# A hybrid decoder layer on one core: more warm-up matmuls, and the first input products ahead of the second half's transposes

## The chip, the cores and the metric

The kernel runs on one core of a Trainium2 chip. The metric is the device time of one execution in microseconds, as the median of the runs shown. The engines are TensorE (PE; its weight loads are listed as PEld), VectorE (DVE), ScalarE (ACT), GpSimd (POOL) and SyncE (SP), whose queue issues the loads from memory here.

## What is computed

One decoder layer on 512 tokens of width 1024, in float32. Two kinds of heads work beside each other, both fed by one input product:

```
h = rms_norm(x, norm_w)                     # (512, 1024)
proj = h @ w_in                             # (512, 4096): hq hf hi hg | aq ak av ag
o_h = rms_norm(hgrn2(hq, hf, hi, lower_bounds)) * silu(hg)     # 4 heads of 128
o_a = moba(aq, ak, av, q_norm_w, k_norm_w) * silu(ag)          # 8 heads of 64
x = x + concat(o_h, o_a) @ w_out
```

HGRN2 is a gated linear recurrence, evaluated in chunks; MoBA is causal attention over blocks of 256 keys with learned choice of past blocks.

## The kernel before

**Products in three parts.** Every float32 product with weights is made of rounded parts: of an operand the kernel keeps a rounded high part and the remainder as a low part (`whi`, `wlo` for weights, `hTh`, `hTl` for the transposed x), and adds high x high, low x high and high x low in PSUM. A chunk of weights is 256 rows by 512 columns (512 KB). ACT makes `whi` (a cast, L109), DVE makes `wlo` (a subtraction, L117). The factor of the RMSNorm over x (`rst`) is put on after the product; `norm_w` is put on at the transposing.

**The opening.** The first group of 512 output columns is `hi`, for which x is the stationary operand: four accumulators, one for each 128 tokens. x comes in by eight loads (128 tokens by 512 columns each) and is transposed on PE. The order on PE in this opening is written out by hand in the string `SEQ` (L128), whose words are:

- `yN`: N matmuls of a 128x128 tile of ones with itself, whose result nobody reads (`warm_up`, L238). Each leaves two records in the trace. The tile they write is one of the two PSUM buffers that the accumulators also use.
- `nt`: `norm_w` into a column, by a small transpose.
- `tAK`: four transposes of x, of token half A (0 is tokens 0 to 255, 1 is 256 to 511) and weight chunk K (256 of the 1024 input columns); behind them two ACT copies of 256 columns into `hTh` (`x_turn`, L248). `lAK` is the pair of DVE instructions for `hTl` (`x_lo`, L261).
- `whK`, `wlK`: the high and the low part of weight chunk K (L105, L113).
- `pUK`: four matmuls of accumulator U (tokens 128 U to 128 U + 127) with `whi` of chunk K; `qUK`: the two with `wlo` (`part`, L832).
- `sqI`: the sum of squares of 128 tokens of x on ACT; `rs`, `rr`: the norm factor, and it as a row; `cv`, `cm`: small constants.

The order on PE is that of the string, word for word. For ACT, DVE and POOL the string is only the order of the program: there a scheduler may let an instruction that is ready earlier go ahead of others. The loads on SP have a string of their own, `DSEQ` (L129): first x of tokens 0 to 255, columns 0 to 511 (`x00`, `x10`), with the first weight chunk (`w0`) behind them, then tokens 256 to 511 (`x20`, `x30`), and so on.

**The rest.** After the opening a planner in the kernel (`drive`) places the other products' matmuls on PE as filler, and between them the steps of the recurrence and of attention, by estimated latencies. The evacuation of the group `av` is `ev_v` (L577): for each 128 tokens one ACT copy into `vt`. Attention comes after it; per unit DVE adds the bias and takes the minimum, ACT applies the exp (L622), DVE takes the reciprocal of the sums (L625), POOL scales (L627), PE transposes. Beside attention runs the output product, whose results DVE adds to x (L697), loaded anew. ACT reads its functions from tables; where the next function isn't in the loaded one, the trace shows an ACT_TABLE_LOAD. `warm` is a tile of one column whose exp has no other use than to have the table loaded.

Of the kernel before, what the change touches and what calls it, by code (L numbers as in the profile page):

```python
# [11 lines left out]
AF = mybir.ActivationFunctionType  # L12
# [9 lines left out]
def kernel(  # L22
# [12 lines left out]
    nc = tc.nc  # L35
# [89 lines left out]

    POOL_LO = (3,)
    LAT = dict(lm=4.544, lev0=9.2567, lev=4.4882, copy=1.9908, rms=5.7036, silu=15.1764, qk=14.2881, soft=2.5598, softn=0.0041, acopy=4.5215, st=1.5748, ch=6.6909, DEPTH=2)
    SEQ = 'y7 nt t00 wh0 t01 sq0 t10 l00 t11 wl0 p00 q00 l01 wh1 p10 q10 l10 p30 q30 wl1 t03 l11 p20 q20 t12 t02 sq1 p01 q01 wh2 l03 l12 sq3 wh3 p21 q21 p11 q11 sq2 l02 p31 q31 wl2 p32 q32 rs wl3 p02 q02 p22 q22 cv t13 p12 q12 rr cm l13'  # L128
    DSEQ = 'x00 nw x10 w0 x20 x30 x01 x31 x11 w1 x21 w2 w4 v w3 w5'  # L129
    POOL_LO = (3,)  # L130
    for w in DSEQ.split():
# [18 lines left out]
    warm = const.tile([P, 1], F32, name="warm")  # L150
# [65 lines left out]
    rst = const.tile([P, NT], F32, name="rst")  # L216
# [328 lines left out]
    A = {}  # L545

    def wait_for(*keys):
        while not all(kk in done for kk in keys):
            advance()
# [27 lines left out]
    def ev_v(u, ps):  # L577
        if u == 0:
            wait_for(*[("read", n) for n in range(NT)])
            A["v"] = big.tile([P, NT, 512], F32, tag="G", name="vt")  # L580
        if u == 1:
            nc.scalar.activation(warm, warm, AF.Exp)
        nc.scalar.activation(A["v"][:, u, :], ps, AF.Copy, scale=rst[:, u:u + 1])


    UNITS = ((3,), (2,), (1, 0))
# [230 lines left out]
    def fill_a():  # L817
        const_tri()
        yield from group(1, True, ev_f)
        yield from group(2, True, ev_silu_t(q2[:, 0]))  # L820
        yield from group(3, False, ev_silu(G))
        yield from group(4, True, ev_silu_t(gT))
        const_dist()
        yield from group(5, False, ev_qk("K", ("f", "k", "i", "KL"), kgs))
        yield from group(6, False, ev_qk("Q", ("q",), qgs))
        yield from group(7, False, ev_v)

    with tc.manual_schedule(engines={mybir.EngineType.PE}):
        with tc.manual_schedule():
# [17 lines left out]
            def part_lo(u, kp):  # L847
# [3 lines left out]
                        wh=split_hi, wl=split_lo)  # L851
            for w in SEQ.split():
                name = w.rstrip("0123456789")
# [58 lines left out]
```

## Time and profile before

| | us |
|---|---|
| median of 3 runs | 296.12 |
| lowest and highest | 296.12 and 297.62 |
| the profiled execution, its own time | 296.24 |
| its span, first to last instruction | 294.5 |
| PE busy | 285.4 (97%) |
| DVE busy | 173.2 (59%) |
| ACT busy | 131.7 (45%) |
| POOL busy | 57.8 (20%) |

The profile is of one execution. Times within it count from the start of the span. A row of a timeline has its start, its duration and its count of merged instructions; what stands in brackets at the end is the idle time of the engine just ahead of the row, with what ended it. Matmuls are pipelined, so a row's duration overlaps the next one; the time of one in a run is the distance of the starts. The granted clock is given as a share of TensorE's full 2.4 GHz; the lower level is 1.2 GHz, 0.50.

### The profile page before, as it was taken

The page shows a single profiled execution, that of the slowest core. Times are in us where ns is not written, and L with a number is a line of the kernel's source. Part 1 is how long each engine was busy: PE and PEld are TensorE (multiplying, and loading weights), DVE is VectorE, ACT ScalarE, POOL GpSimd, SP SyncE. Part 2 cuts the span into 40 slices and gives each one's busy share as a digit, 9 for nine tenths or more (in the row PEclk, how much of TensorE's full clock was granted, in tenths as well). Part 3 has the DMA queues.
Part 4 walks back from the last instruction along what each step waited for, and adds up shares of the span by engine and source line. Part 5 has one row for each costly group of instructions (what it writes and reads, how often), then busy time and mean ns, then how long its engine had stood idle before and what let it go on. Part 6 is the DMA issues. An engine that isn't in the chain of part 4 may idle for free.

```text
span 294.5 us, 5056 instructions
## 1 busy us (share of the span) xinstructions
PE 285.4 (97%) x1945; PEld 236.8 (80%) x1945; DVE 173.2 (59%) x371; ACT 131.7 (45%) x241; POOL 57.8 (20%) x92
## 2 busy tenths in 40 slices
PE   6699999999999999999999999999999999999995
PEld 5588788888877787888888888888887888887884
DVE  4452644464599999446875586485385577633232
ACT  3746654431520456314521653554468697642000
POOL 1003301155000000010254422420004655320000
PEclk9599999999999999999999999999999999999999
DMA  6963276080070006200430089648269000000122
GB/s 202 354 246 129 11 61 250 0 265 21 18 268 6 2 2 198 90 0 0 156 131 1 0 239 185 142 140 226 53 171 341 9 2 0 2 2 2 71 109 105
DMA packets 21642, 31.00 MB, mean 105 GB/s; under 512 B 1509, under 2 KB 8434, under 8 KB 21618
## 3 DMA queue, kind: packets, MB, share of 16 engines
q1 hardware_dynamic: 21618, 30.68, 35.7%
q8 instruction: 15, 0.25, 0.3%
q14 instruction: 9, 0.07, 0.1%
HBM read 25.17 MB, written 2.10 MB: 93 GB/s over the span
## 4 chain that ended last, share of the span: by engine, by line
PE 93%; DMA 5%; SPq 1%; DVE 0%; POOL 0%; issue 0%; DVEq 0%; POOLq 0%
PE acc L173 74%; PE tp L177 7%; PE ot L173 3%; PE sc L173 3%; PE pl L173 3%; DMA x<-in_x_dram 3%; DMA res<-in_x_dram 2%; PE ops L173 2%; PE us L173 1%; SPq L71 0%; DVE res L697 0%; POOL scr L627 0%; SPq L100 0%; DVE res L733 0%; SPq L133 0%
## 5 line engine op out<-in xcount | busy, mean ns | idle before, releaser
L173 PE MATMUL acc<-whi,hTh 128*128 128x512 f32 x160 | 65.4, 409 | 0.0
L173 PE MATMUL acc<-whi,hTl 128*128 128x512 f32 x160 | 63.0, 394 | 0.0
L173 PE MATMUL acc<-wlo,hTh 128*128 128x512 f32 x160 | 60.2, 393 | 0.0
L117 DVE TENSOR_TENSOR wlo<-raw,whi 128x1024 fp32r<-128x1024 f32 x39 | 47.2, 1235 | 13.0 <-ACT whi L109 12.8
L109 ACT CAST whi<-raw 128x1024 fp32r<-128x1024 f32 x40 | 41.5, 1049 | 14.3 <-DMA raw<-in_w_in_dram 6.8
L173 PE MATMUL acc<-hTh,whi 128*128 128x512 f32 x96 | 38.2, 397 | 0.0
L173 PE MATMUL acc<-hTh,wlo 128*128 128x512 f32 x96 | 37.5, 391 | 0.0
L173 PE MATMUL acc<-hTl,whi 128*128 128x512 f32 x96 | 37.4, 389 | 0.0
L163 POOL TENSOR_TENSOR r<-v,mh 128x8 f32<-128x8 f32 (+1 forms) x12 | 17.2, 1430 | 99.5 <-DVE v L161 99.4
L173 PEld LDWEIGHTS acc<-whi,hTl 128*128 128x128 f32 x160 | 30.4, 190 | 6.5
L173 PEld LDWEIGHTS acc<-whi,hTh 128*128 128x128 f32 x160 | 30.5, 191 | 6.3
L173 PEld LDWEIGHTS acc<-wlo,hTh 128*128 128x128 f32 x160 | 30.4, 190 | 5.9
L627 POOL TENSOR_SCALAR scr<-scr,rl 128x512 f32<-128x512 f32 (+3 forms) x32 | 17.7, 564 | 40.7 <-DVE rl L625 37.1
L173 PEld LDWEIGHTS acc<-hTh,wlo 128*128 128x128 f32 x96 | 18.0, 188 | 4.0 <-DVE wlo L117 0.2
L173 PEld LDWEIGHTS acc<-hTl,whi 128*128 128x128 f32 x96 | 18.1, 188 | 3.5
L173 PEld LDWEIGHTS acc<-hTh,whi 128*128 128x128 f32 x96 | 18.0, 188 | 3.6
L173 PE MATMUL acc<-whi,mTa 128*128 128x512 f32 (+1 forms) x72 | 20.4, 367 | 0.0
L697 DVE TENSOR_TENSOR res<-acc,res 128x512 f32<-128x512 f32 x15 | 10.3, 690 | 15.9 <-PE acc L173 14.6
L177 PE MATMUL tp<-ident,scr 128*128 128x128 f32 x128 | 18.6, 276 | 0.4 <-POOL scr L627 0.3
L622 ACT ACTIVATE scr<-scr,nm 128x512 f32<-128x512 f32 (+3 forms) x32 | 17.7, 554 | 2.9 <-DVE nm L619 2.9
L177 PEld LDWEIGHTS tp<-ident,scr 128*128 128x128 f32 x128 | 14.8, 140 | 4.0 <-POOL scr L627 1.1
L619 DVE CUSTOM_DVE_ANT_0 scr<-sc,bias 128x512 f32<-128x512 f32 (+3 forms) x32 | 14.1, 485 | 5.9 <-PE sc L173 5.8
(139 smaller groups left out, 422.0 us busy)
## 6 DMA issues: line engine op xcount, KB each, us to landing
raw<-in_w_in_dram SPq DMA_DIRECT2D x32, 512.0 KB, 4.0
raw<-in_w_out_dram SPq DMA_DIRECT2D x8, 512.0 KB, 3.9
x<-in_x_dram SPq DMA_DIRECT2D x8, 256.0 KB, 7.1
res<-in_x_dram SPq DMA_DIRECT2D x8, 256.0 KB, 6.3
out_dram<-res SPq DMA_DIRECT2D x7, 256.0 KB, 2.1
K<-K SPq DMA_DIRECT2D x8, 128.0 KB, 6.4
KL<-KL SPq DMA_DIRECT2D x8, 128.0 KB, 6.6
Q<-scr SPq DMA_DIRECT2D x8, 128.0 KB, 2.7
```

Source lines behind the costliest of these rows:

```text
L109: nc.scalar.copy(hi, raw)
L117: eng.tensor_sub(lo, raw, hi.bitcast(F32))
L163: nc.gpsimd.tensor_tensor(r, v, mh[:, 0:n], op=ALU.pow)
L173: nc.tensor.matmul(o, a, b, start=start, stop=stop)
L177: nc.tensor.transpose(o, a, ident)
L619: nc.vector.tensor_tensor_reduce(out=z[:, o:o + n], in0=sc[:, o:o + n], in1=bias[:, j, T - n:T], op0=ALU.add, op1=ALU.min, scale=1.0, scal ...
L622: nc.scalar.activation(z[:, o:o + n], z[:, o:o + n], AF.Exp, bias=nm[:, e:e + 1], scale=-1.0, accum_out=l[:, e:e + 1])
L627: nc.gpsimd.tensor_scalar(z[:, o:o + n], z[:, o:o + n], rl[:, e:e + 1], 1.0, op0=ALU.mult, op1=ALU.mult)
L697: nc.vector.tensor_tensor(res[hf][:, u, :], ps, res[hf][:, u, :], op=ALU.add)
```

## The change

Two edits. In `SEQ` the first warm-up grows from 7 to 10 matmuls; one more stands behind the transposes t00 and two behind t01. The words p00 and p10 come ahead of t10, so the first eight products of tokens 0 to 255 stand ahead of the transposes of tokens 256 to 511; q00 stands behind t10, and q10 behind t11. t03 goes behind p20 and q20, and sq0 in the program from behind t01 to behind t03. In `ev_v` the exp on `warm` comes behind the copy of the second tile of `vt` instead of ahead of it, and reads a column of that tile with scale 0.

```
-    SEQ = 'y7 nt t00 wh0 t01 sq0 t10 l00 t11 wl0 p00 q00 l01 wh1 p10 q10 l10 p30 q30 wl1 t03 l11 p20 q20 t12 t02 sq1 p01 q01 wh2 l03 l12 sq3 wh3 p21 q21 p11 q11 sq2 l02 p31 q31 wl2 p32 q32 rs wl3 p02 q02 p22 q22 cv t13 p12 q12 rr cm l13'
+    SEQ = 'y10 nt t00 wh0 y1 t01 l00 y2 p00 wl0 p10 l01 t10 q00 t11 q10 l10 wh1 p30 q30 l11 wl1 p20 q20 t03 sq0 t12 t02 sq1 p01 q01 wh2 l03 l12 sq3 wh3 p21 q21 p11 q11 sq2 l02 p31 q31 wl2 p32 q32 rs wl3 p02 q02 p22 q22 cv t13 p12 q12 rr cm l13'
...
         if u == 0:
             wait_for(*[("read", n) for n in range(NT)])
             A["v"] = big.tile([P, NT, 512], F32, tag="G", name="vt")
+        nc.scalar.activation(A["v"][:, u, :], ps, AF.Copy, scale=rst[:, u:u + 1])
         if u == 1:
-            nc.scalar.activation(warm, warm, AF.Exp)
-        nc.scalar.activation(A["v"][:, u, :], ps, AF.Copy, scale=rst[:, u:u + 1])
+            nc.scalar.activation(warm, A["v"][:, u, 0:1], AF.Exp, scale=0.0)
```

PE at the start of the program, before: x_79 holds tokens 0 to 255 of x, x_80 tokens 256 to 511; `wp` is what the warm-up writes, `tp` what a transpose writes, `acc` an accumulator.

```order
L241 MATMUL wp<-scr 128x128 x7
L245 MATMUL tpn<-ident,vec 128x8
L177 MATMUL tp<-ident,x_79 128x128 x8
L177 MATMUL tp<-ident,x_80 128x128 x8
L173 MATMUL acc<-whi,hTh 128x512
L173 MATMUL acc<-whi,hTl 128x512
```

The same place on PE after the change, up to t11:

```order
L241 MATMUL wp<-scr 128x128 x10
L245 MATMUL tpn<-ident,vec 128x8
L177 MATMUL tp<-ident,x_79 128x128 x4
L241 MATMUL wp<-scr 128x128
L177 MATMUL tp<-ident,x_79 128x128 x4
L241 MATMUL wp<-scr 128x128 x2
...
L173 MATMUL acc<-whi,hTh 128x512
L173 MATMUL acc<-whi,hTl 128x512
L177 MATMUL tp<-ident,x_80 128x128 x4
L173 MATMUL acc<-wlo,hTh 128x512 x2
L177 MATMUL tp<-ident,x_80 128x128 x4
```

The eight matmuls of p00 and p10 (the first six of them are left out) have moved ahead of the transposes of x_80, and the transposes of x_80 now have a pair of `wlo` products between them.

ACT at the start, the difference: `raw_85` holds the first two weight chunks, `raw_94` the third; `sq` is a sum of squares.

```order
 L258 ACTIVATE hTh<-tp,nwc 128x256 x2
+L109 CAST whi<-raw_85 128x1024
+L258 ACTIVATE hTh<-tp,nwc 128x256 x6
 L109 CAST whi<-raw_85 128x1024
 L258 ACTIVATE hTh<-tp,nwc 128x256 x2
 L223 ACTIVATE sq,ssx<-x_79 128x1024
 L258 ACTIVATE hTh<-tp,nwc 128x256 x4
-L109 CAST whi<-raw_85 128x1024
-L258 ACTIVATE hTh<-tp,nwc 128x256 x6
 L223 ACTIVATE sq,ssx<-x_79 128x1024
 L109 CAST whi<-raw_94 128x1024
```

The first sum of squares has moved from ahead of the copies of t10 and t11 to behind the second weight chunk and the copies of t03.

ACT between the group `av` and the first softmax, before:

```order
L583 ACTIVATE vt<-acc,rst 128x512
L535 ACTIVATE Q<-tp,qgs 64x4x128 x2
L583 ACTIVATE vt<-acc,rst 128x512
L535 ACTIVATE Q<-tp,qgs 64x4x128
L109 CAST whi<-raw 128x1024 x3
L583 ACTIVATE vt<-acc,rst 128x512
L109 CAST whi<-raw 128x1024
L622 ACT_TABLE_LOAD
L622 ACTIVATE scr,l<-scr,nm 128x512 x2
```

And after the change, from the second tile of `vt` on:

```order
L581 ACTIVATE vt<-acc,rst 128x512
L535 ACTIVATE Q<-tp,qgs 64x4x128
L583 ACT_TABLE_LOAD
L583 ACTIVATE warm<-vt 128x1
L535 ACTIVATE Q<-tp,qgs 64x4x128
L581 ACTIVATE vt<-acc,rst 128x512
...
L109 CAST whi<-raw 128x1024
L622 ACTIVATE scr,l<-scr,nm 128x512 x2
```

The table load has moved from in front of the first exp of attention to between two copies of Q. On DVE at that place one of the two reciprocals of the second unit has moved ahead of the residual add that they both stood behind. SP's order is the same.

## Rows read from the trace of the kernel before

**Rows 1.** The page, part 1: busy us, share of the span, instructions per engine.
```profile
PE 285.4 (97%) x1945; PEld 236.8 (80%) x1945; DVE 173.2 (59%) x371; ACT 131.7 (45%) x241; POOL 57.8 (20%) x92
```

**Rows 2.** Who PE waited for: us in total, times, longest.
```profile
PE tp L177 <- DMA x<-in_x_dram: 4.3, 3, 3.5
```

**Rows 3.** The chain of waits that ended last: start, us, what.
```profile
2.96 7.57 DMA x<-in_x_dram
...
19.53 0.87 PE tp L177 x8
...
32.20 49.78 PE acc L173 x219
...
120.57 0.89 PE ops L173 x8
```

**Rows 4.** Timeline of PE, 0 to 22 us: start, us, what, idle before.
```profile
1.04 3.35 PE L241 MATMUL wp<-scr 128*128 128x128 f32 x14 [1.04 <-DVE warm L151]
4.32 0.27 PE L245 MATMUL tpn<-ident,vec 8*128 8x8 f32 x1
...
5.20 0.99 PE L177 MATMUL tp<-ident,x 128*128 128x128 f32 x7 [0.33 <-DMA x<-in_x_dram]
9.71 0.45 PE L177 MATMUL tp<-ident,x 128*128 128x128 f32 x1 [3.52 <-DMA x<-in_x_dram]
10.57 1.76 PE L177 MATMUL tp<-ident,x 128*128 128x128 f32 x7 [0.42 <-DMA x<-in_x_dram]
11.98 0.78 PE L173 MATMUL acc<-whi,hTh 128*128 128x512 f32 x1
...
13.84 1.05 PE L173 MATMUL acc<-wlo,hTh 128*128 128x512 f32 x2
14.69 0.47 PE L173 MATMUL acc<-whi,hTh 128*128 128x512 f32 x1
...
20.16 0.47 PE L173 MATMUL acc<-whi,hTh 128*128 128x512 f32 x1
```

**Rows 5.** PE by stretches: from:to, length, PE busy, granted clock, DMA share, GB/s.
```profile
4.50:8.00 3.50, 1.36 (x9) 1.00 0.96 297
8.00:9.70 1.70, 0.00 (x0) 0.51 0.97 311
...
12.00:14.80 2.80, 2.80 (x9) 0.50 0.93 356
14.80:20.20 5.40, 5.40 (x32) 1.00 0.60 206
```

**Rows 6.** Timeline of ACT and DVE in the opening.
```profile
5.79 0.84 ACT L258 ACTIVATE hTh<-tp,nwc 128x256 fp32r<-128x256 f32 x2 [3.34 <-PE tp L177]
...
6.66 0.87 DVE L266 SCALAR_TENSOR_TENSOR hTl<-tp,nwc,hTh 128x256 fp32r<-128x256 f32 x2
...
8.08 1.04 ACT L109 CAST whi<-raw 128x1024 fp32r<-128x1024 f32 x1 [1.46 <-DMA raw<-in_w_in_dram]
...
21.45 1.07 ACT L223 ACTIVATE sq<-x 128x1024 f32<-128x1024 f32 x1
...
22.49 1.06 ACT L109 CAST whi<-raw 128x1024 fp32r<-128x1024 f32 x1
...
23.58 1.23 DVE L117 TENSOR_TENSOR wlo<-raw,whi 128x1024 fp32r<-128x1024 f32 x1 [1.04 <-ACT whi L109]
```

**Rows 7.** Timeline of ACT, DVE and PE around the exp tables and the first softmax.
```profile
2.24 0.20 ACT L582 ACTIVATE warm<-warm 128x1 f32<-128x1 f32 x1
...
209.76 0.68 ACT L535 ACTIVATE Q<-tp,qgs 64x512 fp32r<-64x512 f32 x1 [3.12 <-PE tp L177]
...
220.16 1.28 ACT L622 ACT_TABLE_LOAD   x1
...
224.47 0.69 DVE L697 TENSOR_TENSOR res<-acc,res 128x512 f32<-128x512 f32 x1 [1.30 <-DMA res<-in_x_dram]
...
225.97 1.11 PE L177 MATMUL tp<-ident,scr 128*128 128x128 f32 x6 [0.34 <-POOL scr L627]
```

## The prediction, made before the changed kernel ran

> **What bounds the kernel now.** The page comes first: TensorE (PE) is busy 285.4 us, 97% of the span [rows 1], so only two things can shorten the span: the 9 us in which it stands idle, and work done at a lower clock. The list of who waited for whom says where PE stood: 4.3 us for loads of x [rows 2]; beside that 1.04 us ahead of the first warm-up matmul [rows 4], 0.34 us for GpSimd (POOL) late in the kernel [rows 7], and some 3.4 us at the end, while the last output goes out. The chain of waits confirms it: until 10.53 us the end of the kernel hangs on a load of x, and from there on almost without a break on PE [rows 3]. So whatever moves the first long run of matmuls forward moves the end by as much, unless something behind it is not ready. The timeline shows the opening: the transposes of tokens 0 to 255 (t00, t01) end at 6.19 (5.20 + 0.99), then PE waits 3.52 us and, after one transpose, 0.42 us more for the x rows of tokens 256 to 511; p00 starts at 11.98 [rows 4]. The third view is the granted clock: 1.00 up to 8 us, 0.50 to 14.8, then 1.00 again [rows 5]. It fell about 1.8 us after PE went idle and came back at 14.8, after 2.8 us of unbroken matmuls. Under it a matmul took 0.425 us (two from 13.84 to 14.69) [rows 4] against 0.2273 (49.78 / 219) at the full 2.4 GHz [rows 3], and a transpose 0.201 (10.57 to 11.98 for seven) against 0.109 (0.87 / 8) [rows 3, 4]. The clock view's 1.00 before 4 us I don't trust: 14 warm-up records took 0.234 us each (1.04 to 4.32) [rows 4], where the same 128x128 f32 form takes 0.111 (0.89 / 8) later [rows 3].
>
> So the stretch from 6.19 to the start of p01 at 20.16 lasts 13.97 us, but holds only 24 matmuls and 20 transposes: 24 x 0.2273 + 20 x 0.109 = 5.46 + 2.18 = 7.63 us at full level. Of the 6.3 us above that, 3.9 is waiting and about 2.4 the clock.
>
> **The reordering.** What p00 and p10 need is there before the x rows of tokens 256 to 511: the rounded weight whi of the first chunk is finished by ScalarE (ACT) at 8.08 + 1.04 = 9.12, bound by the load of that chunk, which this change doesn't touch (SP issues the same loads in the same order and waits there for earlier loads only); hTh and hTl of t00 were ready by 7.53 [rows 6]. So p00 can start at about 9.18 and stand where PE now waits. All that follows up to p01 is the same 24 matmuls and 20 transposes. At the full level p01 starts at 9.18 + 7.63 = 16.81. One new hand-over could hold it: p30 needs hTl of t10, which VectorE (DVE) makes after ACT's pair. At full level t10 ends at about 11.6, ACT's pair takes 0.84, DVE's first half 0.44 more [rows 6]: 12.9 to 13.0, and p30 comes up at 9.18 + 12 x 0.2273 + 8 x 0.109 = 12.78, its hTl matmul 0.23 later. That is level, and I put 0.1 on it. p01 at 16.9, **3.26 us earlier** than 20.16. From p01 on PE's order is unchanged, and the rest shifts as a block.
>
> **The warm-up matmuls.** Six are added, 12 records, at 0.111 to 0.234 each: 1.3 to 2.8 us. They end by 6.19 + 2.8 = 9.0 at the worst, still ahead of 9.18: cost nothing, hidden by the load of the first weight chunk. Without that cover they would cost their 1.3 to 2.8. The six records ahead of t00 (0.7 to 1.4 us) push its transposes; ACT's pair then ends by about 7.4 instead of 6.63, still ahead of the 8.08 at which ACT turns to the weight. What they change is the idle hole: before, from 6.19 to 9.71; now from 7.5 to 9.0 until 9.18, 0.2 to 1.7 us.
>
> **The clock** is the unknown. I take it that it stays full: the hole ahead of p00 is at most 1.7 us, where it was 3.52, and behind it come eight matmuls in place of a transpose and another wait. The other end, a fall at 8 us as before, is priced below: each us spent at half level costs half a us.
>
> **ACT's and DVE's queues.** sq0 leaves its place ahead of the t10 pair, and now stands behind the t03 pair, ahead of the t12 and t02 pairs and of the third weight chunk. With t03's transposes done at about 16.1: pair 0.84, sq0 1.04 (21.45 to 22.49), two pairs 1.68, sq1 1.04, whi 1.05: whi of the third chunk at 21.75, wlo 1.23 later at 23.0 [rows 6]. PE asks for them at 16.9 + 24 x 0.2273 = 22.36 and, for wlo, four matmuls later, at 23.27. Slack 0.6 and 0.27: nothing lost, but narrow. Before, they came at 23.54 and 24.81, asked for at 25.6 and 26.5.
>
> **The exp.** Before, the second exp on "warm" ran at 2.24 us, long ahead of the sigmoids that need another table, so the exp table was loaded in front of the first softmax, 1.28 us at 220.16. Now it is tied to the second v tile, and the load falls between two Q copies, where ACT idled 3.12 us before the copy at 209.76: 1.28 + 0.20 fits. The softmax starts 1.3 us earlier. That frees PE only where PE waited for it: 0.34 us at 225.97, behind POOL, behind DVE, whose reciprocals were queued behind a residual add that waited 1.30 us for its load [rows 7]. One of the two reciprocals now stands ahead of that add, the other still behind. Bounds 0 and 0.34; a loss is excluded while the 3.12 us idle covers 1.48. I take **0.3**, since one of two transposed tiles comes free and its transposes fill the other's wait.
>
> **Sum.** The profiled run took 296.24 us, 294.5 span and 1.74 outside it. 296.24 - 3.26 - 0.3 = 292.68; the median of the runs lies 0.12 lower, so **292.6 us**.
>
> **The rivals.**
> A, the forecast: full clock from p00 on, 292.6. For it: the hole shrinks from 3.5 to under 1.7 us. Against: before, the clock fell with 1.36 us of PE work between 4.5 and 8.0 [rows 5], and no row shows how much more would have held it. Chance 0.60.
> B: the clock falls at 8 us all the same and returns, as before, after 2.8 us of unbroken matmuls: p00 and p10 are such a run (8 x 0.425 = 3.4), so it is low from 9.18 to 12.0. Cost 2.8 / 2 = 1.4: 294.0. Chance 0.14.
> C: it falls and returns at the same moment as before, 14.8: cost 5.6 / 2 = 2.8, so 295.4, within 0.5% of now (which is about what a measurement of this kernel can tell from no change). Chance 0.10.
> D, slower: it falls, and because p00 and p10 are now followed by transposes between q00 and q10, the unbroken run that raises it starts only at p30. At half level p30 comes at 9.18 + 12 x 0.425 + 8 x 0.201 = 15.9, the rise 2.8 later at 18.7; cost 9.5 / 2 = 4.8, so 297.4. It decides against the change from a return later than 16.3 us (3.56 x 2 behind 9.18). Against it: in the old order too seven transposes stood ahead of the run. Chance 0.06.
> The Trainium skill, "TensorE: Matmul & The Clock Gate", Part 4 (PE-mode transpose), says that the full clock doesn't engage for transposes, as they don't count as work in the same way; by that rule the transposes among the added matmuls would help little and D would be the outcome. The trace agrees only in part: eight transposes at 19.53 ran at 0.109 us each under a granted 1.00 [rows 3, 5]; whether transposes hold the clock, no row shows.
> E: the gain is there, but PE catches up with ACT and DVE at the third chunk (p32, q32). Price from 0 to 0.8, one squaring of 1.04 less the slack of 0.27: 293.4. Chance 0.10.
> That the change doesn't do what it says (p00 not free to start before the x rows) would need the first weight chunk to land 2.5 us later than at 8.08; its issue stands ahead of them on SP, so I give that nothing of its own.
>
> **How the numbers follow.** Under 294.6 (0.5%) lie A, E and most of B: faster 0.82. C, the upper part of B and half of D: same 0.15. The rest of D: slower 0.03. The range starts at 291.8: A with both terms at their best is 292.4, and the runs shown drift by more than 0.6. It ends at 295.0, past B, and leaves out most of C and all of D.
>
> **What would show it.** In the new profile: p00 at 9.1 to 9.3 and p01 near 16.9 on PE; a granted clock of 1.00 from 8 to 15 us (a 0.50 there means B to D, and its end tells which); no wait of PE for ACT or DVE around 22 to 23 us (E); the exp table load near 203 to 205 and no wait of PE for POOL near 222. The prediction is wrong if the clock falls, or if PE waits for a weight chunk afterwards by more than 1 us.

## The result, and the profile after

The changed kernel takes 292.53 us (median of 6 runs, 292.03 to 293.66) against 296.12 (6 runs, 294.63 to 297.62). The ratio is 0.9884, 95% interval 0.9853 to 0.9914. Forecast were 292.6 and a range from 291.8 to 295.0. The profiled execution has a span of 290.9 us, 3.6 less than before. Ratios and intervals, here and in the table below, leave out the executions in a second, slower state (two of order only, and seven and two of the kernel before in the first two groups) and are not the quotients of the medians.

The page of the changed kernel, PE's line of part 1 and the granted clock in 40 slices (tenths):

```profile
PE 285.0 (98%) x1957; PEld 237.3 (82%) x1957; DVE 174.6 (60%) x371; ACT 131.5 (45%) x241; POOL 57.9 (20%) x92
...
PEclk9999999999999999999999999999999999999999
```

PE is busy for as long as before [rows 1], with 12 records more, in a span that is 3.6 us shorter. No slice here falls below 9, where before the clock stood at 0.50 from 8.0 to 14.8 us [rows 5].

The opening, timeline of the changed kernel (start, us, what, idle before):

```profile
1.04 4.64 PE L241 MATMUL wp<-scr 128*128 128x128 f32 x20 [1.04 <-DVE warm L151]
...
7.45 0.61 PE L241 MATMUL wp<-scr 128*128 128x128 f32 x4
...
8.04 1.04 ACT L109 CAST whi<-raw 128x1024 fp32r<-128x1024 f32 x1 [0.24 <-DMA raw<-in_w_in_dram]
...
9.13 0.50 PE L173 MATMUL acc<-whi,hTh 128*128 128x512 f32 x1 [1.08 <-ACT whi L109]
...
17.00 0.48 PE L173 MATMUL acc<-whi,hTh 128*128 128x512 f32 x1
...
20.64 1.08 ACT L109 CAST whi<-raw 128x1024 fp32r<-128x1024 f32 x1
...
21.76 1.23 DVE L117 TENSOR_TENSOR wlo<-raw,whi 128x1024 fp32r<-128x1024 f32 x1 [1.05 <-ACT whi L109]
...
22.57 0.39 PE L173 MATMUL acc<-whi,hTh 128*128 128x512 f32 x1
...
23.48 0.61 PE L173 MATMUL acc<-wlo,hTh 128*128 128x512 f32 x2
```

The answer to [rows 4]: the hole of 3.52 + 0.42 us is now one of 1.08 us, and it waits for the first weight chunk instead of for x. p00 starts at 9.13, p01 at 17.00: 3.16 us earlier than 20.16. The third chunk's whi and wlo end at 21.72 and 22.99 and are asked for at 22.57 and 23.48: no wait, with 0.85 and 0.49 us to spare. The stretches of PE show why the 7.87 us from p00 to p01 are so short (length, PE busy, granted clock, DMA share, GB/s; compare [rows 5]):

```profile
4.50:8.00 3.50, 3.50 (x21) 1.00 0.95 303
8.00:9.70 1.70, 0.62 (x3) 1.00 1.00 327
...
12.00:14.80 2.80, 2.80 (x15) 1.00 0.94 358
```

Who PE waited for in the whole changed kernel (us, times, longest):

```profile
PE acc L173 <- ACT whi L109: 1.1, 1, 1.1
PE wp L241 <- DVE warm L151: 1.0, 1, 1.0
PE tp L177 <- POOL scr L627: 0.3, 1, 0.3
```

The wait for POOL is still there, though the exp table now comes early. The timeline around the first softmax (score matmuls start at 213.95, the filler behind the second unit at 224.26: 10.31 us; before 217.10 to 227.84, 10.74 us):

```profile
203.52 1.28 ACT L583 ACT_TABLE_LOAD   x1
```

```profile
220.37 1.03 PE L177 MATMUL tp<-ident,scr 128*128 128x128 f32 x8
...
222.11 0.51 PE L177 MATMUL tp<-ident,scr 128*128 128x128 f32 x3
222.95 0.55 PE L177 MATMUL tp<-ident,scr 128*128 128x128 f32 x3 [0.32 <-POOL scr L627]
```

The filler is the next matmul of another product, the first behind the transposes and score matmuls of that unit. Three of the six transposes no longer wait; the other three do, as [rows 7] had all six. What they wait for, on DVE:

```profile
221.38 0.69 DVE L697 TENSOR_TENSOR res<-acc,res 128x512 f32<-128x512 f32 x1 [2.48 <-DMA res<-in_x_dram]
221.98 0.15 DVE L625 RECIPROCAL rl<-l 128x1 f32<-128x1 f32 x1
```

The residual add waits for x, and the reciprocal that POOL needs stands behind it. The 3.6 us of the span are the 3.16 of the opening and the 0.43 here.

### The profile page after: what moved, and what is told of

Its sections match the earlier page's. It is cut to its first block, busy times and chain, and to the rows that moved or that the text cites. A ratio compares the mean times of both kernels' runs of the same rounds, so it can differ in the third digit from the quotient of the medians.

```text
span 290.9 us, 5079 instructions
## 1 busy us (share of the span) xinstructions
PE 285.0 (98%) x1957; PEld 237.3 (82%) x1957; DVE 174.6 (60%) x371; ACT 131.5 (45%) x241; POOL 57.9 (20%) x92
## 4 chain that ended last, share of the span: by engine, by line
PE 95%; DMA 2%; SPq 0%; ACT 0%; POOL 0%; DVE 0%; issue 0%
PE acc L173 76%; PE tp L177 6%; PE sc L173 3%; PE ot L173 3%; PE pl L173 3%; PE ops L173 2%; DMA raw<-in_w_in_dram 2%; PE us L173 1%; ACT whi L109 0%; SPq L71 0%; POOL scr L627 0%; DVE res L733 0%; SPq L133 0%; PE tpv L794 0%; PE rp L232 0%
## 5 line engine op out<-in xcount | busy, mean ns | idle before, releaser
L173 PE MATMUL acc<-whi,hTh 128*128 128x512 f32 x160 | 64.7, 404 | 1.1 <-ACT whi L109 1.1
L697 DVE TENSOR_TENSOR res<-acc,res 128x512 f32<-128x512 f32 x15 | 10.3, 689 | 17.1 <-PE acc L173 14.6
L177 PEld LDWEIGHTS tp<-ident,scr 128*128 128x128 f32 x128 | 14.8, 140 | 3.6 <-POOL scr L627 0.7
```

Of the source, the lines that this page charges most:

```text
L173: nc.tensor.matmul(o, a, b, start=start, stop=stop)
L177: nc.tensor.transpose(o, a, ident)
L697: nc.vector.tensor_tensor(res[hf][:, u, :], ps, res[hf][:, u, :], op=ALU.add)
```

## The experiments

They ran in three groups, each on one chip and beside the kernel before on that chip: 294.65 us in the first group, 294.90 in the second, 294.93 in the third. In most profiles there the loads of x and of the first weights land earlier than in the first one (ACT's cast of the first weight chunk starts between 6.86 and 7.72 us instead of 8.04, but at 8.56 in the long warm-up). Times are compared within a group only. p00 and p01 are the first product and the first product of the second weight chunk on PE, each in the one profiled execution, whose time can stand at either end of its kernel's runs (warm-ups only: 295.10 of 292.08 to 295.10; ten in front only: 291.54 of 291.54 to 293.45).

| kernel | group | median us | of before | 95% interval | p00 | p01 |
|---|---|---|---|---|---|---|
| order only | 1 | 294.31 | 0.9966 | 0.9930 to 1.0001 | 8.82 | 19.23 |
| warm-ups only | 1 | 293.12 | 0.9960 | 0.9933 to 0.9988 | 10.55 | 18.98 |
| exp only | 1 | 294.53 | 1.0007 | 0.9985 to 1.0030 | 10.29 | 18.94 |
| all transposes | 1 | 292.74 | 0.9944 | 0.9912 to 0.9976 | 8.62 | 16.49 |
| changed kernel again | 2 | 293.05 | 0.9926 | 0.9893 to 0.9960 | 7.95 | 15.86 |
| ten in front only | 2 | 292.76 | 0.9933 | 0.9901 to 0.9964 | 7.97 | 15.83 |
| long warm-up | 2 | 293.97 | 0.9967 | 0.9938 to 0.9996 | 10.32 | 18.17 |
| first chunk early | 2 | 292.12 | 0.9904 | 0.9870 to 0.9939 | 8.15 | 16.06 |
| no residual | 3 | 291.55 | 0.9886 | 0.9838 to 0.9933 | 8.59 | 16.45 |
| exp undone | 3 | 293.22 | 0.9945 | 0.9922 to 0.9968 | 8.58 | 16.47 |
| old order, filled | 3 | 294.28 | 0.9987 | 0.9963 to 1.0012 | 11.34 | 18.18 |
| more squares | 3 | 294.47 | 1.0001 | 0.9970 to 1.0033 | 8.60 | 16.47 |

**The order without the warm-ups.**

```
-    SEQ = 'y10 nt t00 wh0 y1 t01 l00 y2 p00 wl0 p10 ...'
+    SEQ = 'y7 nt t00 wh0 t01 l00 p00 wl0 p10 ...'
```

> The new order of products and transposes and the new place of the exp, but 7 warm-up matmuls at the start and none among the transposes, as before. PE should then idle from about 6.2 to 9.13 us. Theory 1 (the extra warm-up matmuls are what holds the clock): the granted clock falls to 0.50 near 8 us as before and stays there for 2.8 to 5.6 us of work, p01 starts 1.4 to 2.8 us later than the 17.0 of the changed kernel, time 293.9 to 295.3. Rival (the order alone does it, a hole of 2.9 us is short enough): clock 1.00 throughout, p01 at 17.0, 292.5.

Its opening by PE, and its stretches:

```profile
8.82 0.80 PE L173 MATMUL acc<-whi,hTh 128*128 128x512 f32 x1 [2.78 <-ACT whi L109]
9.41 0.63 PE L173 MATMUL acc<-whi,hTl 128*128 128x512 f32 x1
9.84 0.63 PE L173 MATMUL acc<-whi,hTh 128*128 128x512 f32 x1
...
19.23 0.48 PE L173 MATMUL acc<-whi,hTh 128*128 128x512 f32 x1
```

```profile
4.50:8.00 3.50, 1.30 (x9) 0.97 0.89 290
8.00:9.70 1.70, 0.88 (x2) 0.50 1.00 323
...
12.00:14.80 2.80, 2.80 (x13) 0.53 0.99 376
```

Theory 1 holds. With a hole of 2.78 us the clock falls just ahead of 8 us, p00 and p10 run at 0.43 us a matmul, and full speed returns only at about 14.6. From p00 to p01 it takes 10.41 us instead of 7.87: the 2.5 us that the clock takes back. What the order wins by starting at 8.82 it thus mostly loses; 0.9966 of before can hardly be told from 1. This is the prediction's case C, in the profiled execution (294.92 us): the twelve runs go from 290.92 to 295.68, and what the clock did in the opening of the others is not shown.

**The warm-ups without the order.**

```
-    SEQ = 'y7 nt t00 wh0 t01 sq0 t10 ...'
+    SEQ = 'y10 nt t00 wh0 y1 t01 y2 sq0 t10 ...'
```

> The old order and the old exp, with only the six extra warm-up matmuls (10 at the start, 1 behind t00, 2 behind t01). PE still waits for x until 10.57 us. Theory 1 (hole and clock are separate losses): the hole shrinks to 0.7 to 2.4 us, the clock stays at 1.00, and after 10.57 us 24 matmuls (5.46) and 19 transposes (2.07) at full level put p01 at 18.1 instead of 20.16: 2 us gained, 294.1. Rival (the warm-ups are of no use without the order, since PE still idles around 8 to 10 us): clock falls as before, p01 near 20.2, 296.1.

PE, and the granted clock in narrow stretches (in that view PEld, DVE, ACT and POOL stand between PE's busy time and the clock):

```profile
8.78 0.30 PE L177 MATMUL tp<-ident,x 128*128 128x128 f32 x1 [1.65 <-DMA x<-in_x_dram]
9.82 0.98 PE L177 MATMUL tp<-ident,x 128*128 128x128 f32 x7 [0.73 <-DVE wlo L117]
```

```profile
10.50:11.00 0.50, 0.50 (x5) 0.46 (x4) 0.43 (x4) 0.42 (x1) 0.00 (x0) 1.00 1.07 414
11.00:11.20 0.20, 0.20 (x3) 0.11 (x2) 0.07 (x1) 0.20 (x1) 0.00 (x0) 0.59 1.08 420
11.20:11.40 0.20, 0.20 (x2) 0.20 (x1) 0.00 (x0) 0.20 (x1) 0.00 (x0) 0.50 1.03 399
```

In this execution neither side had it right. The warm-ups carry the clock past 8 us, but PE then idles 1.65 and 0.73 us, and the clock falls at 11.1, when PE has been busy again for more than a microsecond. So idle time can be paid for later. But the profiled execution is the one with the longest time, 295.10 us; the other eleven runs lie between 292.08 and 293.89. By its median, 293.12, the kernel is 1.5 us below before, not far from the 2 us of theory 1, 1.2 below the order only and just 0.4 above all transposes below (292.74), which has the new order, the new place of the exp and transposes as its warm-ups, on the same chip and with an overlapping interval. So in the times the warm-ups alone come close to the whole change; how much the order adds to them is not settled.

**The exp alone, and the exp undone.** The first is the kernel before with the edit of `ev_v`, the second the changed kernel without it:

```
+        nc.scalar.activation(A["v"][:, u, :], ps, AF.Copy, scale=rst[:, u:u + 1])
         if u == 1:
-            nc.scalar.activation(warm, warm, AF.Exp)
-        nc.scalar.activation(A["v"][:, u, :], ps, AF.Copy, scale=rst[:, u:u + 1])
+            nc.scalar.activation(warm, A["v"][:, u, 0:1], AF.Exp, scale=0.0)
```

> Only the exp on warm behind the second v tile. Theory 1: opening as before; in the first softmax PE gains what it gained in the changed kernel, 0.2 to 0.45 us, so 295.7 to 295.9; seen in the distance from the first score matmul to the first filler matmul behind the second unit's transposes, 10.9 before and 10.3 to 10.5 here. Rival: nothing but noise, 296.1, and the 0.44 us came with the other timing of the loads.

> The changed kernel with the exp on warm back in its old place. Theory 1: opening as in the changed kernel; the exp table load is back in front of the first softmax, and from the first score matmul to the filler behind the second unit's transposes PE takes 0.4 us more, beside what it waits for POOL: 0.4 us slower than the changed kernel, less than a median can show. Rival (the exp is worth nothing, the 0.4 us are the timing of loads): the distance without the wait for POOL is 9.97 to 10.0 as with the new place.

PE in the first softmax, exp only:

```profile
222.38 1.03 PE L177 MATMUL tp<-ident,scr 128*128 128x128 f32 x8
...
225.55 0.55 PE L177 MATMUL tp<-ident,scr 128*128 128x128 f32 x3 [0.91 <-POOL scr L627]
```

and with the exp undone in the changed kernel:

```profile
220.19 1.43 PE L177 MATMUL tp<-ident,scr 128*128 128x128 f32 x8 [0.19 <-POOL scr L627]
...
223.14 1.11 PE L177 MATMUL tp<-ident,scr 128*128 128x128 f32 x6 [0.65 <-POOL scr L627]
```

From the first score matmul to the filler it took 10.89 us with the exp moved (215.97 to 226.86), of which 0.91 waiting for POOL; 11.58 with it undone (213.43 to 225.01), of which 0.84. Less those waits that is 9.98 and 10.74; the changed kernel's first profile gives 9.99, before 10.40. The other kernels bear it out: 10.56 and 10.74 with the old place (warm-ups only; old order, filled), 9.76 to 9.99 with the new one wherever the clock stayed full. So the edit takes 0.4 to 0.75 us off PE's way through the first softmax, and what PE waits for POOL, 0.3 to 0.9 us in these, has another cause. In the medians neither shows: 1.0007 for the exp only, and 0.9945 with it undone, on another chip than the changed kernel's 0.9926.

**All warm-ups as transposes.**

```
+    def turn_up(n):
+        wp = pacc.tile([P, 512], F32, tag="acc", name="wp")
+        for _ in range(n):
+            nc.tensor.transpose(wp[:, 0:P], ones, ident)
...
-    SEQ = 'y10 nt t00 wh0 y1 t01 l00 y2 p00 ...'
+    SEQ = 'z20 nt t00 wh0 z2 t01 l00 z4 p00 ...'
```

The new word `zN` stands for N of these transposes (`turn_up`).

> The changed kernel with each of its warm-up matmuls replaced by as many 128x128 f32 transposes of the ones tile as it left records (20, 2 and 4), so PE has only transposes until p00. Theory 1 (transposes hold the clock as matmuls do): p00 and p10 at 0.23 us a matmul, p01 at 17.0, 292.5. Rival (transposes don't count, as the Trainium skill, TensorE: Matmul & The Clock Gate, Part 4, says): the matmuls of p00 and p10 take 0.425 us each from the start, the clock is full only after some 2.8 us of them or later, p01 1.4 to 4.8 us later, 294 to 297.

```profile
1.44 4.53 PE L241 MATMUL wp<-ident,scr 128*128 128x128 f32 x20 [1.44 <-DVE sbit L778]
...
6.81 0.60 PE L177 MATMUL tp<-ident,x 128*128 128x128 f32 x4
7.24 0.60 PE L241 MATMUL wp<-ident,scr 128*128 128x128 f32 x4
8.62 0.50 PE L173 MATMUL acc<-whi,hTh 128*128 128x512 f32 x1 [0.77 <-ACT whi L109]
8.95 0.39 PE L173 MATMUL acc<-whi,hTl 128*128 128x512 f32 x1
9.18 0.39 PE L173 MATMUL acc<-whi,hTh 128*128 128x512 f32 x1
```

Theory 1 again: after nothing but transposes the first products come 0.23 us apart, and p01 follows p00 by 7.87 us, as in the changed kernel. The first 20 took 0.22 us each (1.44 to 5.90), the four of t01 0.108 each (6.81 to 7.24): by then the level had risen. So f32 transposes of 128x128 raised the clock here and held it. The Trainium skill, "TensorE: Matmul & The Clock Gate", Part 4 (PE-mode transpose), says the opposite, that the full clock does not engage for them; the measurement decides.

**The changed kernel again, and the three among the transposes.** The first is the changed kernel as it is; the second drops `y1` and `y2`, so that PE idles 1.43 us instead of 0.76.

```
-    SEQ = 'y10 nt t00 wh0 y1 t01 l00 y2 p00 wl0 ...'
+    SEQ = 'y10 nt t00 wh0 t01 l00 p00 wl0 ...'
```

> The changed kernel itself, unchanged, on the chip of this group, as the measure for the three others. Theory 1: its opening again without a change of the granted clock before 20 us, p00 as soon as the first weight chunk is rounded, p01 7.8 us behind p00. Rival (the first profile was a lucky one): a stretch at 0.50 in the opening, p01 9 to 12 us behind p00.

> The changed kernel without the three warm-up matmuls among the transposes (y1, y2); the ten at the start stay. PE idles from about 7.2 to the first product near 9, 1.7 us instead of 1.1. Theory 1a (it is the length of the hole that matters): clock 1.00 throughout, time as the changed kernel within 0.5 us. Rival 1b (the three are needed): clock 0.50 for 2.8 us or more from about 8 or 11 us on, 1.4 us or more slower.

The opening of both stays at 1.00, and p01 comes at 15.86 and 15.83: theory 1a, the three later warm-ups weren't needed in this execution. The repeated kernel's profile shows something else. Its opening was over 1.1 us earlier than in the first profile, yet its span is 292.7 us. PE there, and its stretches:

```profile
223.17 0.79 PE L177 MATMUL tp<-ident,scr 128*128 128x128 f32 x3 [1.67 <-POOL scr L627]
223.61 0.78 PE L173 MATMUL sc<-K,Q 128*128 128x512 f32 x1
```

```profile
223.20:224.00 0.80, 0.80 (x4) 0.58 0.67 246
224.00:226.60 2.60, 2.60 (x7) 0.50 0.09 32
```

The wait for POOL is 1.67 us, and behind it the clock falls to 0.50 for 3.4 us (223.3 to 226.7). From the first score matmul to the filler it takes 12.64 us (212.83 to 225.47) instead of 10.31, and the half level goes on beyond that. The span of the ten in front, with the same opening and a wait of 0.30 us at this place, is 289.8.

**No residual.** What the three transposes wait for: POOL scales by a reciprocal that stands on DVE behind the residual add, and that add waits for x to be loaded anew [rows 7]. The edit, with the function's other lines left out:

```
-            for z in range(NT):
-                nc.sync.dma_start(out=res[hf][:, z, :], in_=xv[:, z, cs])
-        nc.vector.tensor_tensor(res[hf][:, u, :], ps, res[hf][:, u, :], op=ALU.add)
+        if part == 0:
+            nc.vector.tensor_copy(res[hf][:, u, :], ps)
+        else:
+            nc.vector.tensor_tensor(res[hf][:, u, :], ps, res[hf][:, u, :], op=ALU.add)
```

> The changed kernel with the residual x left out: its eight loads are gone, and the first additions on DVE are copies from PSUM (the output lacks x). Theory 2 (the scatter of the changed kernel and what is left of PE's waiting in the first softmax come from the load of x for the residual add, behind which DVE's reciprocal is queued): no wait of PE for POOL between 215 and 230 us, granted clock 1.00 there, 10.0 us from the first score matmul to the filler behind the second unit's transposes (10.3 in the changed kernel's first profile), 0.3 to 2.5 us faster than the changed kernel and runs closer together. Rival (PE's wait there is ACT's and DVE's own latency): the wait of 0.3 us or more stays, time the same within 0.3 us.

```profile
221.62 0.84 PE L177 MATMUL tp<-ident,scr 128*128 128x128 f32 x6
```

```profile
222.00:230.00 8.00, 8.00 (x64) 1.00 0.00 0
```

The wait is gone, as theory 2 has it: the six transposes run in one go, PE waits for nothing from the score matmuls on, 9.76 us to the filler (213.47 to 223.23), and the clock stays full. By itself that proves little, since all transposes and more squares, which load x, have no wait here either. What settles it is the start of the first residual add on DVE. In the changed kernel again it is

```profile
221.60 0.69 DVE L697 TENSOR_TENSOR res<-acc,res 128x512 f32<-128x512 f32 x1 [3.77 <-PE tp L177]
```

Counted from the first score matmul, over the nine profiles with the exp in its new place and the load:

| kernel | add starts after, us | PE waits for POOL, us |
|---|---|---|
| all transposes | 6.86 | none |
| more squares | 7.02 | none |
| ten in front only | 7.40 | 0.30 |
| changed kernel, first profile | 7.43 | 0.32 |
| order only | 7.46 | 0.36 |
| exp only | 8.01 | 0.91 |
| long warm-up | 8.10 | 1.00 |
| first chunk early | 8.37 | 1.26 |
| changed kernel again | 8.77 | 1.67 |

Beyond 7.1 us the wait grows with the start of the add, us for us. PE runs alike up to there in all nine (the second unit's transposes begin 8.15 or 8.16 us behind the first score matmul), so PE, which the row above names, is not what moves the add; the load of x, named in the first profile's row, is. The changed kernel did not run in this group, so what the load costs it in time is not shown; the exp-undone kernel of the group is 1.7 us slower, of which 0.4 to 0.75 are the exp. Nor is the scatter explained: the four runs here lie within 0.8 us (290.94 to 291.75), but so do, within 0.9, the ten of the exp-undone kernel (292.57 to 293.44), which loads x.

**A long warm-up.**

```
-    SEQ = 'y10 nt t00 wh0 y1 t01 l00 y2 p00 ...'
+    SEQ = 'y10 nt t00 wh0 y1 t01 l00 y14 p00 ...'
```

> The changed kernel with 14 instead of 2 warm-up matmuls behind t01: 24 records more at 0.111 us, 2.7 us. Theory 1 (warm-ups are free only as far as the load of the first weight chunk covers them): p00 starts when they end, near 10.5 to 11 us instead of near 9, and the kernel is 1.6 to 2.0 us slower than the changed one. Rival (something else holds p00 to p01, such as the x loads or the second weight chunk): less than 0.5 us slower.

```profile
7.28 3.29 PE L241 MATMUL wp<-scr 128*128 128x128 f32 x28
10.32 0.48 PE L173 MATMUL acc<-whi,hTh 128*128 128x512 f32 x1
```

p00 comes when the warm-ups end, 2.4 us later than in the repeated kernel, and p01 2.3 later. Only a part of this is the warm-ups' doing: the first weights came late in this execution, and ACT's cast of them ended at 9.61 (8.56 + 1.05), so the warm-ups held p00 by 0.7 us. By the medians the kernel is 0.9 us slower than the repeated one, less than the 1.6 to 2.0 expected. What holds the opening is whatever comes last ahead of p00, and warm-ups are free only up to there.

**The first chunk early.**

```
+        wv = src[kp * 256:(kp + 1) * 256, c0:c0 + 512].rearrange("(k p) c -> p k c", p=P)
+        if n == 0:
+            for d in range(2):
+                nc.scalar.dma_start(out=raw[:, d, :], in_=wv[:, d, :])
+        else:
+            nc.sync.dma_start(out=raw, in_=wv)
...
+        if n == 0:
+            for d in range(2):
+                nc.scalar.copy(hi[:, d, :], raw[:, d, :])
...
-    SEQ = '... p20 q20 t03 sq0 t12 t02 sq1 p01 q01 wh2 l03 l12 sq3 wh3 p21 ...'
-    DSEQ = 'x00 nw x10 w0 x20 ...'
+    SEQ = '... p20 q20 t03 t12 t02 p01 q01 wh2 sq0 l03 l12 sq3 wh3 sq1 p21 ...'
+    DSEQ = 'w0 x00 nw x10 x20 ...'
```

> The changed kernel with the first weight chunk loaded in two halves from ACT's queue at the start, rounded in two halves, and the sums of squares sq0 and sq1 behind the third weight chunk on ACT. Theory 1 (what bounds the opening now is the load of that chunk): it lands about 1 to 1.5 us earlier, p00 follows, p01 likewise unless the second chunk (whi at 14.8, wlo at 16.1 in the changed kernel) is late: 0.7 to 1.5 us faster than the changed kernel. Rival (the loads share one bandwidth, so what the weight gains x loses): p00 earlier, but t00 or t10 wait for x, less than 0.3 us gained.

```profile
6.76 0.84 ACT L265 ACTIVATE hTh<-tp,nwc 128x256 fp32r<-128x256 f32 x2 [3.61 <-PE tp L184]
7.49 1.14 ACT L114 CAST whi<-raw 128x512 fp32r<-128x512 f32 x2
```

Neither: the weights were there, the cast follows ACT's copies of t00 without a wait, and those waited for PE, whose first warm-up runs at half level to 5.6 us. p00 came no earlier (8.15 against 7.95). Nor could it: in the repeated kernel too the cast, at 6.86, had followed the copies of t00 without a wait for its load. On this chip, then, the load no longer covers the first ten warm-ups in these two executions; with the weights there, the warm-ups and t00 are themselves the bound. The median is the lowest of its group, 292.12, but its interval overlaps that of the changed kernel; a version that beats it is not shown.

**The old order, filled.**

```
-    SEQ = 'y7 nt t00 wh0 t01 sq0 t10 ...'
+    SEQ = 'y10 nt t00 wh0 y1 t01 y14 sq0 t10 ...'
```

> The old order of products and transposes and the old exp, but with warm-up matmuls (10, 1 and 14) until the x rows of tokens 256 to 511 are there: PE doesn't idle, so the clock should stay full, but the waiting for x is still filled with nothing of use. Theory 1 (hole and clock are separate losses, about 2.4 us for the clock): clock 1.00 in the whole opening, p01 some 2 us earlier than before and 1.2 us later than in the changed kernel, 0.995 of before or 1 to 2 us faster. Rival (the order is what counts, the clock by itself gives little): under 0.5 us faster than before.

```profile
10.55 1.04 PE L177 MATMUL tp<-ident,x 128*128 128x128 f32 x8
11.34 0.48 PE L173 MATMUL acc<-whi,hTh 128*128 128x512 f32 x1
```

The clock stayed full, and from p00 to p01 it took 6.84 us, against 8.65 with the old opening of the exp-only kernel and 8.18 before. But the filler ran to 10.55, while in the exp-only kernel the same transposes began at 8.30. It was too long for these chips, and its time (not told from before) doesn't settle what the clock is worth by itself. It does show what the half level cost from p00 on: 1.3 us before and 1.8 in the exp-only kernel. Beside the exp-undone kernel of its group, which differs from it in the order and in twelve warm-ups fewer, p01 comes 1.7 us later and the median is 1.1 us higher; how much of that is the order and how much the filler that ran too long is not shown.

**More squares.**

```
-    SEQ = '... t03 sq0 t12 t02 ...'
+    SEQ = '... t03 sq0 sq0 sq0 t12 t02 ...'
```

> The changed kernel with the first sum of squares done three times over on ACT, 2.0 us more ahead of the third weight chunk. Theory 1 (ACT's queue ahead of that chunk has 0.5 us to spare): PE waits about 1.1 us for whi at p32 and 0.4 for wlo at q32, 1.5 us later from there on. Rival (more slack than the reading gives, or the wait is made up later): PE waits under 0.5 us, time as the changed kernel.

```profile
23.60 0.50 PE L173 MATMUL acc<-whi,hTh 128*128 128x512 f32 x1 [1.40 <-ACT whi L109]
```

Theory 1, and somewhat more. The cast of the third chunk starts 2.4 us later on ACT than in the exp-undone kernel, which has the same opening (22.50 against 20.11). PE waits 1.40 us at p32, which comes 1.56 us later (23.60 against 22.04), and is held again at q32, behind `wlo`: 1.91 us later (24.86 against 22.95). From there on the lag is 2.0 us. No gain over before is left to be seen (1.0001). So the slack at p32 was about 0.85 us, as in the first profile, and at q32 about 0.5. Case E's mechanism is real; the changed kernel just stays clear of it.

## Why the prediction was right

**p00 at 9.18, bound by the first weight chunk.** Right for the first profile: 9.13, behind a cast from 8.04. On the other chips the copies of t00 or the weights came last, and p00 started between 7.95 and 8.62 in the kernels with the new order and the warm-ups, the long warm-up apart.

**24 matmuls and 20 transposes at full level, p01 at 16.9.** Right: 17.00, 7.87 us behind p00 against 7.73. The hand-over at p30 took about 0.1, as put down.

**The warm-ups cost nothing.** Right in the first profile, hidden until 9.13, but with less to spare than reckoned: all of the first 20 records ran at the half level (4.57 / 20 = 0.23 us), the upper bound of the term for them, ACT's pair ended at 7.80 instead of 7.4, and the cast then waited only 0.24 us for its load. In five later profiles with this order (changed kernel again, ten in front only, all transposes, exp undone, more squares) it did not wait for the load at all: there the warm-ups were no longer wholly covered, and what they cost is not shown. The long warm-up shows a price of 0.7 us beyond the cover.

**The clock stays full.** Right, and this was the uncertain step: 0.60 for A. In the profiles the order alone ran into case C, so the warm-ups are what made A. That the ones among the transposes count is not shown: the ten in front were enough. Rival D lost its ground when transposes alone raised and held the level, and in the order only the level came back at 14.6, ahead of p30 at 15.25 and not 2.8 us behind it.

**The exp, 0.3 us.** The size came near (0.43 measured), but by luck, for the account of it was wrong: the bound of 0.34 was PE's visible wait, and that is still there (0.32). The gain lies in transposes that PE ran as POOL handed them over, 0.98 us for eight before and 0.79 now (start to start), and in three of the next six that no longer wait. The upper bound was too low: 0.4 to 0.75 in the traces.

**The sum.** 3.56 forecast, 3.16 + 0.43 in the spans. What the prediction did not weigh is how far the gain may hang on load times: repeated on another chip, the same pair gives 0.9926 instead of 0.9884, by these ratios 2.2 us instead of 3.4, though the intervals overlap. A likely reason, not shown for that chip, is that the old opening waits less for x there: on a third chip the exp-only kernel, whose opening is the old one, waits 0.90 and 1.73 us instead of 0.33, 3.52 and 0.42, and p01 is at 18.94 instead of 20.16. It also took PE's wait behind the residual load for a fixed 0.34 us; with the new place of the exp it ranges from none to 1.67, and behind the longest the clock fell a second time.

## What to carry to other kernels

Where PE waits for loads at the start, look for products whose operands land first and put them into the hole, and then ask what the remaining hole does to the clock: here the order alone gained almost nothing, and matmuls without a use, which kept the level up, came within 0.4 us of both together in the medians of one chip. So measure the cheap edit by itself first. Count what covers such filler; past the last operand to arrive it is paid for (0.7 us in the long warm-up). And look at what stands on an engine behind an instruction that waits for a load (here a reciprocal behind the residual add), for that is where the next wait came from.

## What was not expected of the hardware

- The granted clock fell at 11.1 us in the kernel with the warm-ups only, after 1.3 us of unbroken work, with idle time before it (1.65 and 0.73 us). A fall needs no idle PE at that moment.
- A hole of 2.78 us (order only) cost the level. Single holes ahead of p00 behind the ten warm-ups did not, from 0.33 us (first chunk early) to 1.64 (no residual, the row below, at a granted 1.00 throughout the opening). One of 1.65 with another of 0.73 behind it did (warm-ups only), and so did one of 1.67 in the middle of the kernel (the changed kernel again), where 1.00 and 1.26 (long warm-up, first chunk early) did not. The length of a hole alone does not tell these apart.
- Transposes and no matmul raised the level, from 0.22 us apiece for the first twenty to 0.108 for the four of t01.
- The granted clock is shown as 1.00 from the start of the span although the warm-up records take twice what they take at full level (0.23 against 0.111 us); before the first change that is shown, durations are the better witness.

The longest hole that kept the level, in the kernel without the residual:

```profile
8.59 0.50 PE L173 MATMUL acc<-whi,hTh 128*128 128x512 f32 x1 [1.64 <-ACT whi L109]
```
